# A hybrid encoder on one core: the second tokens' norm into each mixer is split into x times norm weight ahead of the root and a scaling behind it

## The chip, the cores and the metric

The kernel runs on one core of a Trainium2 chip. The metric is the device time of one execution in microseconds; the time before is the median of three runs.

## What is computed

Two layers over 256 tokens of width 1024, in float32. Each layer is a half-weighted SwiGLU feed-forward (FFN), a mixer with two head groups, and a second FFN; each of the three starts with a root-mean-square norm of the residual `x`:

```python
def rms_norm(x, g):
    x32 = x.astype(jnp.float32)
    y = x32 * lax.rsqrt(jnp.mean(x32 * x32, axis=-1, keepdims=True) + EPS)
    return (y * g.astype(jnp.float32)).astype(x.dtype)

for l in range(DEPTH):
    x = x + FFN_RES * swiglu(rms_norm(x, ffn1_norm[l]), ...)
    h = rms_norm(x, mix_norm[l])
    proj = h @ w_in[l]          # recurrent input, gate, q, k, v
    y = concat(rms_norm(y_rec, ...), rms_norm(y_att, ...))
    x = x + y @ w_out[l]
    x = x + FFN_RES * swiglu(rms_norm(x, ffn2_norm[l]), ...)
return rms_norm(x, final_norm)
```

`y_rec` is a gated linear recurrence over the tokens behind a short convolution, `y_att` windowed attention with four query heads per key head.

## The kernel before, in words

The 256 tokens are two tiles of 128, t = 0 and t = 1; the residual stays in SBUF as `xt[0]`, `xt[1]` of 128x1024. Every float32 product is made of three products of rounded parts: a tile is split into a high part (`xh`, `wh`, a rounding copy by ScalarE) and a low part (`xl`, `wl`, a subtraction by VectorE), and TensorE multiplies high by high, high by low and low by high. Weights come by SyncE's DMAs as raw 1 MB pieces; `prep_one` (L307, L308) splits them into ring slots, a 128x1024 copy on ScalarE and a 128x1024 subtraction on VectorE for each slot, some pieces ahead of their use.

The program is a chain of six stages (FFN, mixer, FFN, twice), and `boundary` joins each to the next. It runs the last part of the old stage's down projection (`tail`) for t = 0, then for t = 1, and puts in between, in this order:

- for t = 0: `evac` adds the finished PSUM halves to `xt[0]` (VectorE, L801 after an FFN), `squares` sums the squares of each half (ScalarE, L519, which writes the squares into the norm's own output tile `xn` as waste), `norm` forms the root (`rstd_of`: VectorE L506, then a power on GpSimd L509) and the normed tile in four 128x256 pieces, x times root times norm weight (VectorE, L526);
- `transposes(0)`: eight 128x128 transposes on TensorE (L544) into two PSUM banks, four high-part copies on ScalarE (L549), four low-part subtractions on VectorE (L551), each for two of the eight 128-wide column blocks k;
- the same for t = 1, then `head(0)`, `transposes(1)`, `head(1)` of the new stage. A mixer's `head` is `natural` (L561): 24 matmuls, three passes over the eight blocks; the first two passes read high parts, the third reads the low parts.

Behind the boundary the mixer goes through a list of steps written out by hand (`ORDER`): projections of 24 matmuls (L569 to L571) with a convolution behind four of them (`conv`, L888 to L891 on VectorE, then L899, L900), the recurrence's gates (L911 to L926), attention logits with a fused add and maximum (L985, L988 on VectorE) and exponentials (L990). The projections and logits share four PSUM banks, `ps_c` and `ps_g` with two buffers each.

TensorE's, SyncE's and GpSimd's instructions run in the order in which the program writes them. Those of ScalarE and VectorE are put in order by a scheduler that goes by its own estimate of when each could start. All of one engine's instructions then run in that fixed order. The pool of `xn` has one buffer, so the tile of t = 1 takes the place of that of t = 0, and whoever writes it waits until `transposes(0)` has read it.

Of the kernel before, what the change touches and what calls it, by code (L numbers as in the profile page):

```python
# [10 lines left out]
AF = mybir.ActivationFunctionType  # L11
ALU = mybir.AluOpType
# [4 lines left out]
DM = 1024  # L17
# [24 lines left out]
MAHEAD = 5  # L42
# [25 lines left out]
def encoder_kernel(  # L68
# [31 lines left out]
    pe, act, dve, pool = nc.tensor, nc.scalar, nc.vector, nc.gpsimd  # L100
# [216 lines left out]
    def prefetch(target):  # L317
        while state["half"] <= min(target, state["cap"], len(halves) - 1):
            j = state["half"]
            n = turns.get(halves[j][0], 0)  # L320
            if n >= SLOTS and ring[n - SLOTS] not in used:
                return
            with ExitStack() as behind:
                for ins in state["behind"]:
                    behind.enter_context(tc.issue_after(ins.ins))
                prep_one()
# [13 lines left out]
    xt = [res_p.tile([128, DM], F32, name=f"x{t}", tag=f"x{t}") for t in range(2)]  # L340
# [12 lines left out]
    gain_t = {}  # L353

    def load_gain(i):
        if i < len(gains):
            g = a_p.tile([128, DM], F32, tag="a", name="gain")
            nc.sync.dma_start(out=g, in_=gains[i].partition_broadcast(128))
            gain_t[i] = g
# [26 lines left out]
    def setup_early():  # L386
        idle = ep_p.tile([128, T], F32R, tag="th", name="idle")
        dve.memset(idle.bitcast(F32), 0.0)
        pi = bank("b")

        def keep_warm(n):
            for _ in range(n):
                pe.matmul(pi[:, 0:T], idle[:, 0:128], idle, start=True, stop=True)

        dve.memset(half_t, -0.5)
        dve.memset(ones_t, 1.0)
        load_x(0)
        rows8 = xn_p.tile([128, DM], F32, tag="xn", name="rows8")[0:KD, 0:128]
        nc.scalar.dma_start(out=rows8, in_=ffn1_norm[0].rearrange("(k c) -> k c", c=128))
        nc.scalar.dma_start(out=eye_t, in_=eye)  # L400
        ps = bank("b")
        keep_warm(WARM)
        pe.transpose(ps[:, 0:KD], rows8, eye_t[0:KD, 0:KD])
        keep_warm(WARM2)
        dve.tensor_copy(out=gcol, in_=ps[:, 0:KD])
# [93 lines left out]
    xn_t = {}  # L499
# [3 lines left out]
    def rstd_of(ss, n):  # L503
        st = st_p.tile([128, 2], F32, tag="rstd", name="rstd")
        if n == 2:
            dve.tensor_scalar(st[:, 0:1], ss[:, 0:1], ss[:, 1:2], EPS, ALU.add, ALU.add)  # L506
        else:
            dve.tensor_scalar(st[:, 0:1], ss[:, 0:1], EPS, None, ALU.add)
        pool.tensor_tensor(out=st[:, 1:2], in0=st[:, 0:1], in1=half_t, op=ALU.pow)  # L509
        return st[:, 1:2]  # L510

    ss_t = {}

    def squares(t, hf):
        if hf == 0:
            ss_t[t] = st_p.tile([128, 2], F32, tag="ss", name="ss")
            xn_t[t] = xn_p.tile([128, DM], F32, tag="xn", name="xn")
        sl = slice(hf * 512, hf * 512 + 512)
        return act.activation(out=xn_t[t][:, sl], in_=xt[t][:, sl], func=AF.Square,  # L519
                              scale=1.0 / math.sqrt(DM), accum_out=ss_t[t][:, hf:hf + 1])  # L520

    def norm(t, gi):
        r = rstd_of(ss_t[t], 2)
        for c in range(0, DM, 256):
            sl = slice(c, c + 256)
            ins = dve.scalar_tensor_tensor(out=xn_t[t][:, sl], in0=xt[t][:, sl], scalar=r, in1=gain_t[gi][:, sl],  # L526
                                           op0=ALU.mult, op1=ALU.mult)
        return ins

    def new_x():  # L530
# [3 lines left out]
    def transposes(t):  # L534
        if t == 0:
            new_x()
        xn = xn_t.pop(t)
        ts_ = slice(t * 128, (t + 1) * 128)
        parts = []
        for hf in range(2):  # L540
            ps = bank("ab"[t])
            for j in range(4):
                k = hf * 4 + j
                pe.transpose(ps[:, j * 128:(j + 1) * 128], xn[:, k * 128:(k + 1) * 128], eye_t)  # L544
                if j % 2:
                    p3 = ps[:, (j - 1) * 128:(j + 1) * 128].rearrange("p (k c) -> p k c", k=2)
                    parts.append((p3, cur["h"][:, k - 1:k + 1, ts_], cur["l"][:, k - 1:k + 1, ts_]))
        for p3, xh, xl in parts:
            i1 = act.activation(out=xh, in_=p3, func=AF.Copy)  # L549
        for p3, xh, xl in parts:  # L550
            i2 = dve.tensor_sub(out=xl, in0=p3, in1=xh.bitcast(F32))  # L551
        return [i1, i2]
# [41 lines left out]
    def front():  # L594
        return tc.high_priority(offset=FRONT)

    def boundary(tail, evac, gi, head, ahead):
        prefetch(ahead)
        state["cap"] = ahead
        state["ahead"] = AHEAD  # L600
        tail(0, 0)
        with front():
            for hf in range(2):
                evac(0, hf)
                squares(0, hf)
            norm(0, gi)
        tail(1, 1)
        with front():
            evac(1, 0)
            transposes(0)  # L610
            squares(1, 0)
        tail(1, 2)
        with front():
            evac(1, 1)
            i1 = squares(1, 1)
            i2 = norm(1, gi)
        prefetch(ahead)
        state["behind"] = [i1, i2]
        state["cap"] = ahead + EARLY
        prefetch(ahead + FORCE)  # L620
        head(0)
        with front():
            state["behind"] = transposes(1)
        state["cap"] = 1 << 30
        prefetch(ahead + FORCE2)
        head(1)
        state["behind"] = []
        if gi % 3 != 1:
            load_gain(gi + 1)
# [61 lines left out]
    def ffn(st, acc_done):  # L691
        gu_ps = {}
        hh_t = {}
        acc = {}
# [139 lines left out]

        if st == (DEPTH - 1, 2):
            tail, evac = dn_cols, acc
        return head if st != (0, 0) else first_head, body, tail, evac

    def mix(l):
        st = (l, 1)  # L840
# [295 lines left out]
                if n == "D":  # L1136
                    load_gain(3 * l + 2)

        return head, body, tail, evac

    engines = mybir.EngineType
    with tc.manual_schedule(engines={engines.PE, engines.SP, engines.Pool}):
        stages = [ffn((0, 0), None)]
        step = {"s": first_squares, "n": first_norm, "T": first_transposes, "m": stages[0][0]()}
        for n, f in (("h", first_split), ("w", first_prep)):
            step[n] = lambda *a, f=f: f(False, *a)
            step[n.upper()] = lambda *a, f=f: f(True, *a)
        with tc.manual_schedule(engines={engines.Activation, engines.DVE}):
            setup_early()
            for _ in range(RAWS + 2):  # L1150
                load_raw()
            for tok in FIRST:
                ins = step[tok[0]](*map(int, tok[1:]))
                if tok in BEHIND:
                    state["behind"].append(ins)
        prefetch(3 + LEAD)
        state["behind"] = [ins]
        prefetch(3 + LEAD2)
        state["behind"] = []
        for s in range(3 * DEPTH):  # L1160
            _, body, tail, evac = stages[s]
            body()
            n = s + 1
            if n == 3 * DEPTH:
                with tc.manual_schedule(engines={engines.Activation, engines.DVE}):
                    finish(tail, evac)
                break
            stages.append(mix(n // 3) if n % 3 == 1 else ffn((n // 3, n % 3), None))
            first = index[(n // 3, n % 3), "kv", 0] if n % 3 == 1 else index[(n // 3, n % 3), "gu", 0]
            boundary(tail, evac, n, stages[n][0], first + (MAHEAD if n % 3 == 1 else 3))  # L1170


_INS = ['x', 'ffn1_norm', 'ffn1_w_gate', 'ffn1_w_up', 'ffn1_w_down', 'mix_norm', 'w_in', 'conv_w', 'conv_b',
# [43 lines left out]
```

## Time and profile before

| | |
|---|---|
| median of 3 runs | 938.15 us (937.98 to 938.85) |
| the profiled execution | 938.13 us, of it 936.4 us in the span |
| TensorE (PE) busy | 926.0 us, 99% of the span |
| VectorE (DVE) busy | 696.8 us, 74% |
| ScalarE (ACT) busy | 544.4 us, 58% |
| GpSimd (POOL) busy | 37.4 us, 4% |
| granted TensorE clock, mean | 0.997 of full speed |

Times in the rows are microseconds from the span's start. PEld is TensorE's weight load, which overlaps the matmuls (PE). A row of the timeline gives start, duration of one or of a merged run, engine, line, operation, output and inputs, shape, count, and in brackets how long the engine idled just before and what released it. A duration overlaps the next instruction's by a little, so distances between starts are shorter than durations.

### The profile page before, as it was taken

The numbers are of one execution on the slowest core, as the hardware profiler recorded it, in microseconds if no ns is written. First come the engines' busy times: TensorE is split into PE (matmuls) and PEld (weight loads), VectorE is DVE, ScalarE is ACT, GpSimd is POOL, SyncE is SP. The second block draws the span as 40 slices with busy tenths as digits, with TensorE's granted clock in tenths as the row PEclk, the third lists the DMA queues.
The fourth block names the chain that finished last, engine by engine and source line by source line (L and its number), as shares of the span: only waits on it lengthen the run. The fifth ranks groups of instructions, "written<-read, shape, count | busy, mean of one in ns | idle before, by whom it ended". The sixth has DMA issues, their size and how long they took to land.

```text
span 936.4 us, 13679 instructions
## 1 busy us (share of the span) xinstructions
PE 926.0 (99%) x5288; PEld 804.9 (86%) x5288; DVE 696.8 (74%) x1213; ACT 544.4 (58%) x1005; POOL 37.4 (4%) x60
## 2 busy tenths in 40 slices
PE   9999999999999999999999999999999999999997
PEld 8888888889988888888888888888999888888885
DVE  6888666769998876666688666666799887666663
ACT  7665555548855655555466555554687575555542
POOL 2300000000010000000030000000000100000000
PEclk9999999999999999999999999999999999999998
DMA  9786956714255755565557666555162576665521
GB/s 310 223 269 219 314 184 203 233 56 151 75 162 201 261 186 180 185 205 195 173 175 237 188 196 195 187 180 180 51 221 68 180 240 202 195 195 181 183 87 45
DMA packets 125009, 172.54 MB, mean 184 GB/s; under 512 B 3925, under 2 KB 108797, under 8 KB 124944
## 3 DMA queue, kind: packets, MB, share of 16 engines
q1 hardware_dynamic: 122192, 166.21, 54.8%
q0 software_dynamic: 2304, 4.87, 1.6%
q8 instruction: 41, 0.67, 0.3%
q10 hardware_dynamic: 448, 0.59, 0.2%
q14 instruction: 24, 0.20, 0.1%
HBM read 170.59 MB, written 3.16 MB: 186 GB/s over the span
## 4 chain that ended last, share of the span: by engine, by line
PE 95%; DVE 2%; ACT 1%; issue 1%; DMA 1%; POOL 0%; SPq 0%; POOLq 0%; DVEq 0%
PE ps_g L581 16%; PE ps_c L581 16%; PE ps_c L580 7%; PE ps_g L580 7%; PE ps_a L590 5%; PE ps_a L592 4%; PE ps_a L591 4%; PE ps_b L591 4%; PE ps_b L592 4%; PE ps_b L590 4%; PE ps_g L706 2%; PE ps_c L706 2%; PE ps_a L1021 1%; PE ps_g L569 1%; PE ps_g L570 1%; PE ps_g L571 1%
## 5 line engine op out<-in xcount | busy, mean ns | idle before, releaser
L308 DVE TENSOR_TENSOR wl<-raw,wh 128x1024 fp32r<-128x1024 f32 (+1 forms) x320 | 367.3, 1156 | 102.3 <-ACT wh L307 98.0
L307 ACT ACTIVATE wh<-raw 128x1024 fp32r<-128x1024 f32 (+1 forms) x306 | 301.9, 999 | 82.8 <-PE ps_b L592 60.5
L581 PE MATMUL ps_c<-xhl,wh 128*128 128x512 f32 x640 | 231.3, 396 | 0.0
L581 PE MATMUL ps_g<-xhl,wh 128*128 128x512 f32 x640 | 231.3, 396 | 0.0
L580 PE MATMUL ps_c<-xhl,wl 128*128 128x256 f32 x560 | 156.2, 279 | 0.0
L580 PE MATMUL ps_g<-xhl,wl 128*128 128x256 f32 x560 | 156.1, 279 | 0.0
L581 PEld LDWEIGHTS ps_c<-xhl,wh 128*128 128x128 f32 x640 | 120.1, 188 | 23.0
L581 PEld LDWEIGHTS ps_g<-xhl,wh 128*128 128x128 f32 x640 | 120.1, 188 | 23.0
L580 PEld LDWEIGHTS ps_c<-xhl,wl 128*128 128x128 f32 x560 | 105.6, 189 | 3.5
L580 PEld LDWEIGHTS ps_g<-xhl,wl 128*128 128x128 f32 x560 | 105.6, 188 | 3.5
L590 PE MATMUL ps_a<-wh,hh 128*128 128x512 f32 x168 | 65.7, 391 | 0.0
L590 PE MATMUL ps_b<-wh,hh 128*128 128x512 f32 x168 | 65.6, 391 | 0.0
L592 PE MATMUL ps_b<-wh,hl 128*128 128x512 f32 x168 | 65.4, 389 | 0.0
L591 PE MATMUL ps_b<-wl,hh 128*128 128x512 f32 x168 | 65.4, 389 | 0.0
L592 PE MATMUL ps_a<-wh,hl 128*128 128x512 f32 x168 | 65.4, 389 | 0.0
L591 PE MATMUL ps_a<-wl,hh 128*128 128x512 f32 x168 | 65.4, 389 | 0.0
L766 ACT ACTIVATE sg<-ps_g 128x256 f32<-128x256 f32 x40 | 15.4, 385 | 63.3 <-PE ps_g L581 63.3
L766 ACT ACTIVATE sg<-ps_c 128x256 f32<-128x256 f32 x40 | 15.3, 383 | 52.5 <-PE ps_c L581 51.6
L767 DVE TENSOR_TENSOR sg<-ps_g,sg 128x256 f32<-128x256 f32 x40 | 17.0, 425 | 32.8 <-ACT sg L766 32.7
L766 ACT ACTIVATE su<-ps_c 128x256 f32<-128x256 f32 x40 | 15.4, 386 | 39.0 <-PE ps_c L581 39.0
L754 ACT ACTIVATE hh<-th 128x256 fp32r<-128x256 f32 x80 | 33.4, 417 | 8.1 <-DVE th L748 7.8
L591 PEld LDWEIGHTS ps_a<-wl,hh 128*128 128x128 f32 x168 | 31.6, 188 | 6.9
(323 smaller groups left out, 1577.9 us busy)
## 6 DMA issues: line engine op xcount, KB each, us to landing
raw<-in_ffn_w_down_dram SPq DMA_DIRECT2D x44, 1024.0 KB, 5.0
raw<-in_ffn_w_gate_dram SPq DMA_DIRECT2D x43, 1024.0 KB, 5.4
raw<-in_ffn_w_up_dram SPq DMA_DIRECT2D x43, 1024.0 KB, 5.4
raw<-in_w_in_dram SPq DMA_DIRECT2D x14, 1024.0 KB, 5.5
raw<-in_w_out_dram SPq DMA_DIRECT2D x8, 1024.0 KB, 7.0
lb<-ld POOLq DMA_DIRECT2D x1, 2048.0 KB, 14.9
bias_t<-lb POOLq DMA_DIRECT2D x1, 1536.0 KB, 12.4
gain<-in_ffn_norm_dram SPq DMA_DIRECT2D x3, 512.0 KB, 4.6
```

What stands on the lines that cost most here:

```text
L307: act.activation(out=h3, in_=src, func=AF.Copy)
L308: dve.tensor_sub(out=l3, in0=src, in1=h3.bitcast(F32))
L569: pe.matmul(dst, wh[:, ks], xh[:, k, t0:t1], start=(k == 0), stop=False)
L580: pe.matmul(dst[:, 0:T], wl[:, ks], x2[:, 0, k, :], start=False, stop=False)
L581: pe.matmul(dst, wh[:, ks], x2[:, :, k, :], start=(k == 0), stop=(k == KD - 1))
L590: pe.matmul(acc[hf], ah[:, ts_], wh[:, cs], start=first, stop=False)
L591: pe.matmul(acc[hf], ah[:, ts_], wl[:, cs], start=False, stop=False)
L592: pe.matmul(acc[hf], al[:, ts_], wh[:, cs], start=False, stop=last)
L706: pe.matmul(ps, x, w[k // 2][p % 2][:, k % 2 * 512:k % 2 * 512 + 512], start=(p == 0 and k == 0), stop=(p == 2 and k == KD - 1))
L754: act.activation(out=hh, in_=src, func=AF.Copy)
L766: act.activation(out=s, in_=ps[:, T:2 * T], func=AF.Copy)
L767: dve.tensor_tensor(out=s, in0=ps[:, 0:T], in1=s, op=ALU.add)
```

## The change

It applies at the two boundaries into a mixer alone (`gi % 3 == 1`), and to t = 1 alone. The squares of t = 1 are written as waste into the PSUM bank whose contents `evac` has just taken out, no longer into `xn`. After each half's `evac`, `gained_x` (L532) forms x times norm weight for that half, 128x512, into `xn`. When the root is there, `norm_gained` scales `xn` in place: three 128x256 pieces on VectorE (L539), the fourth on ScalarE (L541). In all other places `norm` stays. The numbers behind the diff's functions move by 14 to 20 lines in the changed kernel: L549 is L563 there, L551 is L565, L801 is L821, L888 to L891 are L908 to L911, L985 is L1005, L988 is L1008.

```diff
-    def squares(t, hf):
+    def squares(t, hf, junk=None):
...
-        return act.activation(out=xn_t[t][:, sl], in_=xt[t][:, sl], func=AF.Square,
+        return act.activation(out=xn_t[t][:, sl] if junk is None else junk, in_=xt[t][:, sl], func=AF.Square,
                               scale=1.0 / math.sqrt(DM), accum_out=ss_t[t][:, hf:hf + 1])
...
+    def gained_x(t, gi, hf):
+        sl = slice(hf * 512, hf * 512 + 512)
+        dve.tensor_tensor(out=xn_t[t][:, sl], in0=xt[t][:, sl], in1=gain_t[gi][:, sl], op=ALU.mult)
+
+    def norm_gained(t):
+        r = rstd_of(ss_t[t], 2)
+        for c in range(0, DM, 256):
+            o = xn_t[t][:, c:c + 256]
+            if c < DM - 256:
+                ins = dve.tensor_scalar(o, o, r, None, ALU.mult)
+            else:
+                act.activation(out=o, in_=o, func=AF.Copy, scale=r)
         return ins
...
-    def boundary(tail, evac, gi, head, ahead):
+    def boundary(tail, evac, gi, head, ahead, acc):
...
-            squares(1, 0)
+            squares(1, 0, acc and acc[1][0])
+            if acc:
+                gained_x(1, gi, 0)
         tail(1, 2)
         with front():
             evac(1, 1)
-            i1 = squares(1, 1)
-            i2 = norm(1, gi)
+            i1 = squares(1, 1, acc and acc[1][1])
+            if acc:
+                gained_x(1, gi, 1)
+                i2 = norm_gained(1)
+            else:
+                i2 = norm(1, gi)
...
-            boundary(tail, evac, n, stages[n][0], first + (MAHEAD if n % 3 == 1 else 3))
+            boundary(tail, evac, n, stages[n][0], first + (MAHEAD if n % 3 == 1 else 3), acc if n % 3 == 1 else None)
```

What this does to the order is seen on VectorE at the boundary into the first mixer. Before (x_115 is `xt[0]`, x_116 is `xt[1]`; xhl holds the high and low parts of the transposed tile, those of t = 0 come from ps_a and those of t = 1 from ps_b; wl is the low part of a ring slot):

```order
L801 SCALAR_TENSOR_TENSOR x_116<-ps_b,x_116 128x512
L526 SCALAR_TENSOR_TENSOR xn<-x_115,rstd,gain 128x256 x4
L551 TENSOR_TENSOR xhl<-ps_a,xhl 128x2x128 x2
L801 SCALAR_TENSOR_TENSOR x_116<-ps_b,x_116 128x512
L551 TENSOR_TENSOR xhl<-ps_a,xhl 128x2x128 x2
L506 TENSOR_SCALAR rstd<-ss 128x1
L526 SCALAR_TENSOR_TENSOR xn<-x_116,rstd,gain 128x256 x4
L308 TENSOR_TENSOR wl<-raw,wh 128x1024
L551 TENSOR_TENSOR xhl<-ps_b,xhl 128x2x128 x4
```

With the change, the same place:

```order
L821 SCALAR_TENSOR_TENSOR x_116<-ps_b,x_116 128x512
L526 SCALAR_TENSOR_TENSOR xn<-x_115,rstd,gain 128x256 x4
L532 TENSOR_TENSOR xn<-x_116,gain 128x512
L565 TENSOR_TENSOR xhl<-ps_a,xhl 128x2x128
L821 SCALAR_TENSOR_TENSOR x_116<-ps_b,x_116 128x512
L565 TENSOR_TENSOR xhl<-ps_a,xhl 128x2x128
L532 TENSOR_TENSOR xn<-x_116,gain 128x512
L506 TENSOR_SCALAR rstd<-ss 128x1
L565 TENSOR_TENSOR xhl<-ps_a,xhl 128x2x128
L539 TENSOR_SCALAR xn<-xn,rstd 128x256 x3
L308 TENSOR_TENSOR wl<-raw,wh 128x1024
L565 TENSOR_TENSOR xhl<-ps_a,xhl 128x2x128
```

The four low-part subtractions of t = 0 stood in pairs ahead of L506; now they stand one by one, and the last of them is behind the three scalings and the 128x1024 weight subtraction. At the boundary into the second mixer the rows from L532 on are the same; ahead of them, before and now, the four L526 stand before the L801 (L821).

On ScalarE, with the change, in the same boundary (L307 copies a ring slot's high part):

```order
L519 ACTIVATE xn,ss<-x_115 128x512 x2
L519 ACTIVATE ps_b,ss<-x_116 128x512
L563 ACTIVATE xhl<-ps_a 128x2x128 x4
L519 ACTIVATE ps_b,ss<-x_116 128x512
L307 ACTIVATE wh<-raw 128x1024
L541 ACTIVATE xn<-xn,rstd 128x256
L563 ACTIVATE xhl<-ps_b 128x2x128 x4
```

Before, both squares of t = 1 stood together behind the four copies from ps_a; the first now stands ahead of them, and the scaling of the fourth piece stands behind the weight copy.

Further on in the mixer the scheduler also sets a few instructions of VectorE in another order. The place at the third convolution, before (pr, stm: attention logits and their maximum, of which the second row of each pair, with stm alone, is the read of the maximum; xc: the convolution, which reads the projection's bank ps_c):

```order
L988 TENSOR_SCALAR stn<-stm 128x2
L888 TENSOR_SCALAR xc<-ps_c,par 128x256
L308 TENSOR_TENSOR wl<-raw,wh 128x1024
L890 SCALAR_TENSOR_TENSOR xc<-ps_c,par,xc 128x254
L985 ISA pr,stm<-ps_g,bias_t,sink_t 128x256
L985 ISA stm 128x1
L890 SCALAR_TENSOR_TENSOR xc<-ps_c,par,xc 128x255
L985 ISA pr,stm<-ps_g,bias_t,sink_t 128x256
L985 ISA stm 128x1
L891 SCALAR_TENSOR_TENSOR xc<-ps_c,par,xc 128x255
```

With the change, the same place, where the weight subtraction L308 stands just ahead of the first row:

```order
L1008 TENSOR_SCALAR stn<-stm 128x2
L908 TENSOR_SCALAR xc<-ps_c,par 128x256
L1005 ISA pr,stm<-ps_g,bias_t,sink_t 128x256
L1005 ISA stm 128x1
L910 SCALAR_TENSOR_TENSOR xc<-ps_c,par,xc 128x254
L1005 ISA pr,stm<-ps_g,bias_t,sink_t 128x256
L1005 ISA stm 128x1
L910 SCALAR_TENSOR_TENSOR xc<-ps_c,par,xc 128x255
L1008 TENSOR_SCALAR stn<-stm 128x2
L1005 ISA pr,stm<-ps_c,bias_t,sink_t 128x256
L1005 ISA stm 128x1
L911 SCALAR_TENSOR_TENSOR xc<-ps_c,par,xc 128x255
```

One more logits pair and one more L1008 now stand ahead of the convolution's last instruction. TensorE's, GpSimd's and SyncE's instructions stand as before.

## Rows read from the trace of the kernel before

**Rows 1.** The page, engines over the span: busy time, share, instructions
```profile
PE 926.0 (99%) x5288; PEld 804.9 (86%) x5288; DVE 696.8 (74%) x1213; ACT 544.4 (58%) x1005; POOL 37.4 (4%) x60
```

**Rows 2.** Busy time by stretch: both boundaries, the first mixer's two early stretches
```profile
core 0: us, PE busy (x) PEld busy (x) DVE busy (x) ACT busy (x) POOL busy (x), PEclk, DMA share, GB/s
188.00:206.00 18.00, 17.53 (x108) 15.10 (x107) 12.23 (x26) 7.63 (x20) 1.12 (x2) 1.00 0.01 3
206.00:230.00 24.00, 23.96 (x204) 23.23 (x203) 20.61 (x50) 17.59 (x42) 0.00 (x0) 1.00 0.52 175
230.00:262.00 32.00, 32.00 (x279) 31.27 (x278) 31.80 (x76) 25.92 (x63) 0.00 (x0) 1.00 0.26 89
647.00:665.00 18.00, 17.51 (x109) 15.11 (x109) 12.97 (x27) 8.57 (x21) 1.12 (x2) 1.00 0.02 5
```

**Rows 3.** Timeline of the first boundary, up to the root of t = 1
```profile
195.96 1.03 PE L544 MATMUL ps_a<-eye_t,xn 128*128 128x128 f32 x8
196.59 1.21 ACT L549 ACTIVATE xhl<-ps_a 128x256 fp32r<-128x256 f32 x4 [3.75 <-PE ps_a L544]
197.28 0.76 DVE L551 TENSOR_TENSOR xhl<-ps_a,xhl 128x256 fp32r<-128x256 f32 x2 [0.90 <-ACT xhl L549]
197.96 0.68 DVE L801 SCALAR_TENSOR_TENSOR x<-ps_b,x 128x512 f32<-128x512 f32 x1
198.55 0.75 DVE L551 TENSOR_TENSOR xhl<-ps_a,xhl 128x256 fp32r<-128x256 f32 x2
199.30 1.04 ACT L307 ACTIVATE wh<-raw 128x1024 fp32r<-128x1024 f32 x1
199.43 0.21 DVE L506 TENSOR_SCALAR rstd<-ss 128x1 f32<-128x1 f32 x1
199.77 0.54 PEld L561 LDWEIGHTS ps_c<-w_i,xhl 128*128 128x128 f32 x4
```

**Rows 4.** The same timeline, from the norm of t = 1 on
```profile
200.31 1.67 DVE L526 SCALAR_TENSOR_TENSOR xn<-x,rstd,gain 128x256 f32<-128x256 f32 x4 [0.66 <-POOL rstd L509]
200.91 0.54 PEld L544 LDWEIGHTS ps_b<-eye_t,xn 128*128 128x128 f32 x4 [0.60 <-ACT wh L307]
200.94 1.53 PE L544 MATMUL ps_b<-eye_t,xn 128*128 128x128 f32 x8 [0.42 <-DVE xn L526]
201.90 1.22 DVE L308 TENSOR_TENSOR wl<-raw,wh 128x1024 fp32r<-128x1024 f32 x1
202.95 0.57 PEld L561 LDWEIGHTS ps_c<-w_i,xhl 128*128 128x128 f32 x4 [0.21 <-ACT xhl L549]
204.86 0.54 PEld L561 LDWEIGHTS ps_c<-w_i,xhl 128*128 128x128 f32 x4
205.33 0.19 PEld L569 LDWEIGHTS ps_g<-xhl,wh 128*128 128x128 f32 x1
```

**Rows 5.** Instructions of the new kinds elsewhere: count, then ns min/median/max
```profile
L653 DVE TENSOR_TENSOR xn<-x,gain x3: 425/682/692, 921.8 to 928.9; 128x512 f32<-128x512 f32 x2, 128x256 f32<-128x256 f32 x1
L666 ACT ACTIVATE xn<-xn,rstd x2: 709/716/722, 927.9 to 931.3; 128x512 f32<-128x512 f32 x2
```

**Rows 6.** Timeline: four scalings of 128x256 on VectorE in the first norm
```profile
6.39 1.15 DVE L418 TENSOR_SCALAR xn<-x,rstd 128x256 f32<-128x256 f32 x4 [0.67 <-POOL rstd L509]
```

**Rows 7.** Timeline: transposes of t = 1 that wait for nothing, at a boundary into an FFN
```profile
291.26 1.02 PEld L544 LDWEIGHTS ps_b<-eye_t,xn 128*128 128x128 f32 x8
292.12 1.21 ACT L549 ACTIVATE xhl<-ps_b 128x256 fp32r<-128x256 f32 x4
```

**Rows 8.** Timeline of the third convolution in the first mixer
```profile
225.17 1.23 DVE L308 TENSOR_TENSOR wl<-raw,wh 128x1024 fp32r<-128x1024 f32 x1 [0.17 <-ACT wh L307]
226.70 0.47 DVE L985 CUSTOM_DVE_ANT_0 pr<-ps_g,bias_t,sink_t 128x256 f32<-128x256 f32 x1
227.10 0.48 DVE L890 SCALAR_TENSOR_TENSOR xc<-ps_c,par,xc 128x255 f32<-128x255 f32 x1
228.43 0.19 PEld L569 LDWEIGHTS ps_c<-xhl,wh 128*128 128x128 f32 x1 [0.24 <-DVE xc L891]
```

**Rows 9.** Chain of waits at the second boundary: start, us, what
```profile
659.12 0.49 DVE xn L526
659.75 0.74 PE ps_b L544 x4
```

More of the change, by code (lines that the diff above doesn't have):

```diff
@@ L527, in norm @@
                                            op0=ALU.mult, op1=ALU.mult)
+        return ins
+    def gained_x(t, gi, hf):
[9 more added lines that the diff above has]
+                act.activation(out=o, in_=o, func=AF.Copy, scale=r)
         return ins
@@ L836, in ffn @@
             tail, evac = dn_cols, acc
-        return head if st != (0, 0) else first_head, body, tail, evac
+        return head if st != (0, 0) else first_head, body, tail, evac, acc
     def mix(l):
@@ L1137, in body @@
                     load_gain(3 * l + 2)
-        return head, body, tail, evac
+        return head, body, tail, evac, None
     engines = mybir.EngineType
@@ L1160, in encoder_kernel @@
         for s in range(3 * DEPTH):
-            _, body, tail, evac = stages[s]
+            _, body, tail, evac, acc = stages[s]
             body()
```

## The prediction

> **What bounds the kernel now.** I read the page's engine shares first: TensorE is busy for 926.0 of 936.4 us [rows 1]. So nothing is won beside it, and what makes it wait is lost in full, unless a later wait takes it up. Next I read the busy time by stretch around the two places that the change touches [rows 2]. In each boundary into a mixer TensorE is idle for only 0.47 and 0.49 of 18 us. In the mixer behind it there is next to no idle time (23.96 of 24 us, then 32.00 of 32), and VectorE is almost full there (31.80 of 32), while in the boundary it works 12.23 of 18. The reader should see from this that little can be gained, and that VectorE has room in the boundary if its instructions stand in the right order.
>
> Then the timeline of the first boundary [rows 3, 4]. The waits of t = 1 follow one another: L506 at 199.43, then the power on GpSimd, the first L526 at 200.31, and the transposes at 200.94, which TensorE had waited 0.42 us for. They then come in the time of the L526 pieces (1.53 us for eight; 1.02 to 1.03 where nothing is awaited [rows 7], [rows 3]), and the head behind them waits another 0.21 us. If all this went, 0.47 + 0.50 + 0.21, so 1.2 us at a boundary and 2.4 us in all, would be the most that the change can win. The second boundary has the same distances (L526 to the transposes: 0.63 us in both [rows 4, 9]).
>
> **The change, part by part.** I replay the new order of VectorE with the distances between starts of the first boundary.
>
> *The two products ahead of the root.* One product of 128x512 costs about 0.60 us from start to start: it lasts 0.682 to 0.692 us [rows 5], as L801 does, whose successor starts 0.59 us later [rows 3]. The first must wait until the transposes of t = 0 have read `xn`: 195.96 + 1.03 = 197.0. It is followed by the first subtraction L565 at 197.6, which takes 0.35 (two from 197.28 to the next row at 197.96), so the second evacuation starts at 197.95: before, 197.96. Squares and their sum are not late by this; before, VectorE sat idle here for 0.90 us, and that covers the first product. Then L565 at 198.55, the second product at 198.9, L506 at 199.5 instead of 199.43. From L506 to the scaling stay 0.88 us (199.43 to 200.31), so the scaling starts at 200.4, late by 0.1.
>
> *The scaling.* Four scalings take 1.15 us in the first norm [rows 6], so 0.27 a piece: the three end their turn at 201.2, where the four L526 ended theirs at 201.90. The fourth, on ScalarE, stands behind the weight copy L307, which is over at 199.30 + 1.04 = 200.34, so the root lets it start at about 200.45. For 128x512 such a scaling takes 0.71 us [rows 5], so for half of it between 0.36 and 0.71: done by 201.2 at the latest. So all of `xn` is there by about 201.3 instead of 201.98. That is the gain that stands to be had, 0.7 us of it.
>
> *What stands behind the scaling now.* The last of the four subtractions of t = 0 gives the low part of blocks 6 and 7, which the last two matmuls of `head(0)` read. Before, it was over at 199.30 [rows 3], and TensorE came to these matmuls at about 200.3 (the group of four loads from 199.77 lasts 0.54). Now it stands behind the scalings and behind the weight subtraction L308: 201.2, plus 1.15 (1.22 less the overlap [rows 4]), gives a start at 202.35; with the 0.42 that one lasts it is over at 202.8. TensorE stands from 200.3 to 202.8, since the transposes of t = 1 come behind `head(0)` in its program: their first load moves from 200.91 to about 203.1, by 2.2 us. What is queued there is the transposes, then `head(1)`, then the whole mixer.
>
> *What comes back.* The transposes then run without gaps. In the boundary into an FFN the first high-part copy starts 0.86 us after the first load and the fourth ends 1.21 us later [rows 7]; then 18 of the 24 matmuls are left, at 0.1175 (a group of four in 0.47: 204.86 to 205.33). That is 0.86 + 1.21 + 2.1 = 4.2 us to the mixer's first projection; where the two loads ahead of them have nothing queued it may be 4.0. Before, it was 4.42 (200.91 to 205.33). So 203.1 + 4.1 = 207.2 against 205.33: **1.85 us lost at each boundary**, with bounds of 1.6 and 2.1, or **3.7 us** for the two.
>
> *In the mixer.* The evacuation of the third convolution's bank is what TensorE waits 0.24 us for [rows 8]. One more logits reduction, 0.40 us from start to start (226.70 to 227.10), and one small L1008 (below 0.15) now stand ahead of it, while the 0.17 us that L308 waited for ScalarE may go. So 0.3 us more a mixer; bounds are 0 (VectorE gains time while TensorE stands) and 0.7. In all **0.6 us**.
>
> *At nothing:* the squares into PSUM (ScalarE idles for 3.75 us ahead of the copies from ps_a [rows 3]; where they come late, in the second boundary, since the norm of t = 0 stands ahead of the evacuation there, the copies slip a little, beside the tail's last three matmuls); the weight DMA behind the boundary, requested later by as much as TensorE; the boundaries out of the mixers, where the evacuations only change places.
>
> Sum: 3.7 + 0.6 = 4.3 us on the profiled execution's 938.13, which stands 0.02 below the median of 938.15: **942.4 us**.
>
> The replay hangs on VectorE keeping its order. The subtraction L551 of 198.55 was ready at 197.80, when the four copies ended, and still ran behind L801 [rows 3]. The Trainium skill, "PSUM — Partial Sum Buffer", section "Engine vs sequencer instructions", says that the queues of ScalarE, VectorE and GpSimd are strictly first in, first out. By that rule the sum stands; were overtaking possible, the last subtraction would slip in ahead of the scaling and the first rival would hold. The row above agrees with the rule.
>
> **The rivals.** *First, not slower: the last subtraction comes in time, and the shorter scaling is won.* It needs that subtraction done by 200.3; from there on the root decides. The transposes would start at about 200.85, follow the pieces at 0.27 instead of 0.40, and the head would end earlier by 0.4 to 0.6 us, so 1.0 in all: 937.1 us, or up to 940 if the subtraction is late by a part. For it speaks that VectorE has room in the stretch [rows 2] and that the pieces do pace the transposes [rows 4]; against it, the written order. The Trainium skill, "Perfetto Trace Analysis", section "Optimizing Scalar/DVE Operations", says that breaking up instructions may let work be done sooner where VectorE is not full but holds up another engine. By that rule it is this rival that comes about; the trace agrees with both conditions (12.23 of 18 us, and TensorE's 0.42), but no row shows a split that was free of a new order.
>
> *Second, slower still: the new order costs more in the mixers.* VectorE is full there [rows 2], and each convolution frees a bank that TensorE wants soon. If a weight subtraction (1.22 us) gets ahead of such a convolution where none was, with no slack to hide it, a mixer loses 1.2 instead of 0.3 us: 942.4 + 1.8 = 944.2. For it speaks that the wait at the third convolution has no slack already [rows 8]; against it, that there the weight subtraction stood ahead before, too.
>
> **How the numbers follow.** A change of 0.2%, about 1.9 us, is what a measurement of this kernel can tell from none. The forecast has a chance of 0.75 and by its bounds reaches from 938.13 + 3.2 = 941.3 to 938.13 + 5.6 = 943.7. The second rival has 0.14, the first 0.11, of which 0.02 lie beyond 0.2% faster (the most that can be won, 2.4 us, gives 935.7) and 0.07 within 0.2%; the rest of it is above 940.0. So faster 0.02, same 0.07, slower 0.91. I take a little of that back, 0.03 from slower to same, for a stall that the mixers take up in a way I do not see. The range from 940.2 to 944.3 leaves out the first rival and the upper part of the second.
>
> **What would show it.** Right: in both boundaries VectorE's last subtraction from ps_a starts about 202.3 in the first boundary's time, TensorE waits some 2.5 us inside `head(0)` for that line (not for the scaling), the transposes of t = 1 then take about 1.0 us instead of 1.5, and the mixer's first projection starts 1.6 to 2.1 us later. TensorE's idle time between 188 and 206 us rises from 0.47 to about 2.5 to 3 us. Wrong: the wait at the transposes stays on the scaling, or the subtraction runs ahead of the weight subtraction; or the boundary loses what I say and the mixer ends no later than before. If the wait at the third convolution is no longer than 0.24 us, the 0.6 us were wrong; if it is over 1 us, the second rival holds.

## The result, and the profile after

The changed kernel takes **946.19 us** (median of three, 946.14 to 947.72) against 938.15: a ratio of 1.0090, 95% interval 1.0077 to 1.0104. It is slower by 8.0 us, where 4.3 were forecast, and lies above the range given. The profiled execution is the longest of the three, 947.72 us, with 945.9 in the span.

The engines over its span, as [rows 1]:

```profile
PE 929.3 (98%) x5288; PEld 807.8 (85%) x5288; DVE 697.0 (74%) x1215; ACT 545.8 (58%) x1007; POOL 37.5 (4%) x60
```

TensorE has the same 5288 matmuls but is busy for 3.3 us more: some of them ran slower. Busy time by stretch, as [rows 2] (stretch, length, busy time of each engine, PEclk, DMA share, GB/s; the second boundary now comes later):

```profile
188.00:206.00 18.00, 15.75 (x88) 13.55 (x87) 12.13 (x28) 8.30 (x21) 1.11 (x2) 0.95 0.01 4
206.00:230.00 24.00, 23.79 (x198) 23.05 (x198) 17.49 (x37) 14.80 (x33) 0.00 (x0) 0.97 0.49 170
230.00:262.00 32.00, 30.52 (x262) 29.45 (x262) 31.68 (x79) 27.00 (x68) 0.00 (x0) 1.00 0.22 72
652.00:673.00 21.00, 18.72 (x107) 16.54 (x106) 13.62 (x28) 8.72 (x22) 1.11 (x2) 0.92 0.06 15
```

TensorE is idle for 2.25 of the first 18 us (before: 0.47; 2.5 to 3 were forecast) and for 1.48 of the 32 us inside the mixer (before: 0). And PEclk, 1.00 in all four stretches before, is 0.95, 0.97 and 0.92 around the boundaries.

VectorE at the first boundary, as [rows 3, 4] (start, duration, engine, line, operation, what it waited for):

```profile
199.59 0.41 DVE L565 TENSOR_TENSOR xhl<-ps_a,xhl 128x256 fp32r<-128x256 f32 x1
200.33 0.88 DVE L539 TENSOR_SCALAR xn<-xn,rstd 128x256 f32<-128x256 f32 x3 [0.33 <-POOL rstd L509]
201.13 1.21 DVE L308 TENSOR_TENSOR wl<-raw,wh 128x1024 fp32r<-128x1024 f32 x1
202.26 0.41 DVE L565 TENSOR_TENSOR xhl<-ps_a,xhl 128x256 fp32r<-128x256 f32 x1
```

The scaling starts at 200.33 and the last low-part subtraction of t = 0 at 202.26; the replay had said 200.4 and 202.35. TensorE's weight loads there, as [rows 4]:

```profile
202.73 0.30 PEld L575 LDWEIGHTS ps_c<-w_i,xhl 128*128 128x128 f32 x2 [2.38 <-DVE xhl L565]
202.97 0.90 PEld L558 LDWEIGHTS ps_b<-eye_t,xn 128*128 128x128 f32 x8
...
204.93 0.97 PEld L575 LDWEIGHTS ps_c<-w_i,xhl 128*128 128x128 f32 x4
205.78 0.97 PEld L575 LDWEIGHTS ps_c<-w_w,xhl 128*128 128x128 f32 x4
...
208.51 0.19 PEld L583 LDWEIGHTS ps_g<-xhl,wh 128*128 128x128 f32 x1
```

TensorE stands for 2.38 us on the subtraction, as forecast, and the transposes come at 202.97 (forecast: 203.1). But a group of four loads of `head(1)` then takes 0.85 us from start to start instead of 0.47, until 208. The windows of 1 us say why (same columns as above):

```profile
203.00:204.00 1.00, 1.00 (x10) 0.87 (x9) 0.00 (x0) 0.29 (x2) 0.00 (x0) 1.00 0.00 0
204.00:205.00 1.00, 0.96 (x6) 0.85 (x5) 0.60 (x2) 1.00 (x5) 0.00 (x0) 0.60 0.00 0
205.00:206.00 1.00, 1.00 (x7) 1.00 (x7) 0.93 (x4) 0.86 (x1) 0.00 (x0) 0.50 0.03 8
206.00:207.00 1.00, 1.00 (x6) 1.00 (x6) 1.00 (x1) 0.00 (x0) 0.00 (x0) 0.50 0.06 16
207.00:208.00 1.00, 1.00 (x8) 1.00 (x7) 0.12 (x1) 0.00 (x0) 0.00 (x0) 0.69 0.00 0
```

The granted clock fell to half, 1.2 of 2.4 GHz, behind the stall, and stayed there for about 3.4 us. The second boundary shows the same (0.71, 0.50, 0.50, 0.58 from 668 to 672).

The third convolution of the first mixer, as [rows 8], on ScalarE, VectorE and TensorE:

```profile
227.37 1.06 ACT L307 ACTIVATE wh<-raw 128x1024 fp32r<-128x1024 f32 x1 [1.18 <-DMA raw<-in_w_in_dram]
228.46 1.23 DVE L308 TENSOR_TENSOR wl<-raw,wh 128x1024 fp32r<-128x1024 f32 x1 [0.55 <-ACT wh L307]
229.67 0.54 DVE L908 TENSOR_SCALAR xc<-ps_c,par 128x256 f32<-128x256 f32 x1
232.19 0.47 DVE L911 SCALAR_TENSOR_TENSOR xc<-ps_c,par,xc 128x255 f32<-128x255 f32 x1
232.72 0.19 PEld L583 LDWEIGHTS ps_c<-xhl,wh 128*128 128x128 f32 x1 [1.13 <-DVE xc L911]
```

Before, the convolution's first operation (L888 at 224.46) stood ahead of the weight subtraction L308. Now all of it stands behind L308, and so behind a weight DMA that had not landed. TensorE waits 1.13 us for the bank; before, 0.24. The waits of its weight loads in the whole first mixer (line, waited for, us in total, times, longest):

```profile
PEld ps_c L583 <- DVE xc L911: 1.1, 1, 1.1
PEld ps_c L583 <- DVE ge L963: 0.7, 1, 0.7
PEld ps_g L583 <- ACT i_t L940: 0.4, 1, 0.4
PEld ps_c L998 <- DVE ql_t L1136: 0.2, 1, 0.2
```

Two more banks, those of the gelu product (L963) and of the recurrence's gate (L940), are waited for, and a logits operand (L1136) for 0.2 us; before, the same view has of all these only the convolution's bank, at 0.24.

In the second mixer the same weight piece is there in time. The wait at the third convolution there, before and after:

```profile
687.24 0.19 PEld L569 LDWEIGHTS ps_c<-xhl,wh 128*128 128x128 f32 x1 [0.25 <-DVE xc L891]
```

```profile
696.09 0.19 PEld L583 LDWEIGHTS ps_c<-xhl,wh 128*128 128x128 f32 x1 [0.50 <-DVE xc L911]
```

The waits on L963, L940 and L1136 are 0.7, 0.4 and 0.2 us there too. What the first of them comes from is seen on VectorE, before and after:

```profile
709.91 0.40 DVE L943 SCALAR_TENSOR_TENSOR ge<-x,ps_c 128x256 f32<-128x256 f32 x1
710.22 0.69 DVE L935 TENSOR_TENSOR_SCAN i_t<-a_t,i_t 128x256 f32<-128x256 f32 x1
```

```profile
718.88 0.66 DVE L955 TENSOR_TENSOR_SCAN i_t<-a_t,i_t 128x256 f32<-128x256 f32 x1
719.46 0.39 DVE L963 SCALAR_TENSOR_TENSOR ge<-x,ps_c 128x256 f32<-128x256 f32 x1
719.90 0.19 PEld L583 LDWEIGHTS ps_c<-xhl,wh 128*128 128x128 f32 x1 [0.73 <-DVE ge L963]
```

The product that frees the bank stood ahead of the recurrence's second scan (L935); now it stands behind it (L955), and TensorE waits 0.73 us. So the new order is not one of a few instructions at the third convolution: it has other places on VectorE, and on ScalarE inside the mixers too.

### The profile page after: what moved, and what is told of

It reads as the page before. It is cut to its first block, busy times and chain, and to the rows that moved or that the text cites. A ratio compares the mean times of both kernels' runs of the same rounds, so it can differ in the third digit from the quotient of the medians.

```text
span 945.9 us, 13675 instructions
## 1 busy us (share of the span) xinstructions
PE 929.3 (98%) x5288; PEld 807.8 (85%) x5288; DVE 697.0 (74%) x1215; ACT 545.8 (58%) x1007; POOL 37.5 (4%) x60
## 4 chain that ended last, share of the span: by engine, by line
PE 90%; DVE 5%; ACT 2%; issue 1%; DMA 1%; POOL 0%; POOLq 0%; DVEq 0%
PE ps_g L595 16%; PE ps_c L595 16%; PE ps_g L594 7%; PE ps_c L594 7%; PE ps_a L604 4%; PE ps_a L606 4%; PE ps_a L605 4%; PE ps_b L605 4%; PE ps_b L606 4%; PE ps_b L604 4%; PE ps_g L726 2%; PE ps_c L726 2%; PE ps_c L575 1%; PE ps_c L597 1%; PE ps_g L597 1%
## 5 line engine op out<-in xcount | busy, mean ns | idle before, releaser
L308 DVE TENSOR_TENSOR wl<-raw,wh 128x1024 fp32r<-128x1024 f32 (+1 forms) x320 | 367.0, 1156 | 103.4 <-ACT wh L307 98.7
L307 ACT ACTIVATE wh<-raw 128x1024 fp32r<-128x1024 f32 (+1 forms) x306 | 302.2, 1000 | 86.4 <-PE ps_b L606 59.8
```

What stands on the lines that cost most here:

```text
L307: act.activation(out=h3, in_=src, func=AF.Copy)
L308: dve.tensor_sub(out=l3, in0=src, in1=h3.bitcast(F32))
```

## The experiments

Three marks on TensorE sum up every run: the first load of `transposes(0)`, the first load of the mixer's first projection, and the first load of the next FFN's `transposes(0)`. From the first to the second is the boundary, from the second to the third the mixer. All from the profiled executions, in us:

| kernel | boundary 1 | mixer 1 | boundary 2 | mixer 2 |
|---|---|---|---|---|
| before | 9.60 | 78.91 | 9.60 | 78.89 |
| after (947.72) | 12.82 | 80.70 | 12.86 | 80.09 |
| after, again (946.15) | 11.40 | 80.92 | 12.57 | 80.08 |
| weight subtraction behind | 10.26 | 81.04 | 10.25 | 80.11 |
| scalings behind too | 9.17 | 78.89 | 9.16 | 78.89 |
| order alone | 14.52 | 80.68 | 13.54 | 80.09 |
| stall filled, 18 matmuls | 11.39 | 80.10 | 11.39 | 80.11 |

For "after" the four differences sum to 3.22 + 1.79 + 3.26 + 1.20 = 9.5 of the 9.6 us that this execution is longer.

The theory: the whole loss hangs on the place of one subtraction in VectorE's queue, by three ways: TensorE stands for it; the clock falls behind the stall; and the scheduler puts another order into the mixers. (That it does so because it estimates TensorE later is an inference; no run shows its estimates.) The rivals stand in the expectations.

**The weight subtraction behind the last low part.** Of the changed kernel's order, only this pair is swapped in each boundary; the mixers' orders are those of the changed kernel.

```diff
-            transposes(0)
+            subs = transposes(0)
...
-        state["behind"] = [i1, i2]
+        state["behind"] = [i1, i2] + (subs if acc else [])
```

> The changed kernel with one swap on VectorE at each boundary into a mixer: the last low-part subtraction of t = 0 stands ahead of the 128x1024 weight subtraction, still behind the three scalings; every other order, in the mixers too, is the changed kernel's. Theory A (the loss is the late subtraction's stall, the halved TensorE clock behind it, and the mixers' new order, 1.8 and 1.2 us): the subtraction is over at about 201.55, the wait falls from 2.4 to about 1.2 us, the clock stays full, 0.6 us stay lost at each boundary and 3.0 us in the mixers, so about 942.3. Rival C (the mixers lose only as an after-effect of the stall, not by their order): the mixers lose nothing, about 939.3. Rival B (the split itself costs, in work and in ScalarE's quarter): over 943.

Measured: 942.71 us (942.41 to 942.84), ratio 1.0048 (1.0034 to 1.0062). The stall and the transposes behind it:

```profile
201.64 0.30 PEld L575 LDWEIGHTS ps_c<-w_i,xhl 128*128 128x128 f32 x2 [1.24 <-DVE xhl L565]
201.88 0.90 PEld L558 LDWEIGHTS ps_b<-eye_t,xn 128*128 128x128 f32 x8
```

A stall of 1.24 us is left, the clock stays at 1.00, and each boundary costs 0.65 us instead of 3.2. But the mixers still cost 2.13 and 1.22 us, no less than behind the longer stall: their new order is a loss of its own, and not an after-effect of the stall or of the fall.

**The scalings behind the subtractions too.** Both low-part subtractions of blocks 4 to 7 now come ahead of the scaling, as before the change. The order in the mixers then comes out as it was before the change.

```diff
-    def norm_gained(t):
+    def norm_gained(t, last):
...
-                ins = dve.tensor_scalar(o, o, r, None, ALU.mult)
+                with tc.issue_after(last.ins):
+                    ins = dve.tensor_scalar(o, o, r, None, ALU.mult)
```

(with `last=subs[1]`, and the edit above)

> The split as in the changed kernel, but the scalings and the weight subtraction are queued behind the last low-part subtraction of t = 0; with this the order in the mixers comes out as in the kernel before. Theory A: no stall, full clock, the mixers as before, and the shorter scaling is won: 0.4 to 0.6 us at each boundary, so about 937.1. Rival B (the split itself costs): over 943. Rival C says the same as A here.

Measured: 937.29 us (937.24 to 938.37), ratio 0.9992 (0.9983 to 1.0001). VectorE and TensorE at the first boundary:

```profile
199.58 0.74 DVE L566 TENSOR_TENSOR xhl<-ps_a,xhl 128x256 fp32r<-128x256 f32 x2
200.32 0.88 DVE L540 TENSOR_SCALAR xn<-xn,rstd 128x256 f32<-128x256 f32 x3
```

```profile
200.74 1.24 PE L559 MATMUL ps_b<-eye_t,xn 128*128 128x128 f32 x8
204.85 0.19 PEld L584 LDWEIGHTS ps_g<-xhl,wh 128*128 128x128 f32 x1
```

The scaling is not late at all (200.32), since the two subtractions fit into the wait for the root. The transposes take 1.24 us instead of 1.53 and no longer wait for VectorE ahead of them (before: 0.42 us); TensorE still stands 0.25 us in `head(0)` for a low-part subtraction. Each boundary wins 0.43 us, the mixers lose nothing. So by the marks the split itself gains 0.9 us, though the interval of this run still reaches 1.0001; all that the changed kernel lost came from the order.

**The order alone.** The kernel before, without the split, with the last low-part subtraction held back until the boundary's weight subtraction has been issued. In the traces the mixers' order on VectorE and ScalarE is that of the changed kernel.

```diff
         for p3, xh, xl in parts:
...
+        for p3, xh, xl in held:
+            with tc.issue_after(state["sub"].ins):
+                dve.tensor_sub(out=xl, in0=p3, in1=xh.bitcast(F32))
```

> The kernel before, without the split, but the last low-part subtraction of t = 0 is queued behind the 128x1024 weight subtraction at each boundary into a mixer; the order in the mixers then comes out nearly as in the changed kernel. Theory A: the norm's four pieces end later than the three scalings, so the wait is 3.1 us instead of 2.4, the clock is halved behind it, the mixers lose as in the changed kernel: 946.2 + 1.4 = 947.6. Rival B (the split is what costs): within 3 us of the kernel before, about 941.

Measured: 948.89 us (948.52 to 949.85), ratio 1.0113 (1.0097 to 1.0128). The stall, then the window of 1 us in which the clock falls and the first one at half clock (columns as above):

```profile
203.35 0.50 PEld L563 LDWEIGHTS ps_c<-w_i,xhl 128*128 128x128 f32 x2 [3.42 <-DVE xhl L626]
203.79 1.66 PEld L544 LDWEIGHTS ps_b<-eye_t,xn 128*128 128x128 f32 x8
```

```profile
202.00:203.00 1.00, 0.00 (x0) 0.00 (x0) 1.00 (x2) 0.00 (x0) 0.00 (x0) 0.84 0.00 0
203.00:204.00 1.00, 0.65 (x3) 0.65 (x4) 0.29 (x1) 0.00 (x0) 0.00 (x0) 0.50 0.00 0
```

Without any new operation, the one late subtraction costs even more than the change: four L526 pieces stand ahead of it instead of three shorter scalings, the stall is 3.42 us, and the clock, which falls before the stall is over, is at half for some 6.8 us, until 209.5. The mixers lose 1.77 and 1.20 us, as in the changed kernel.

**The stall filled.** The changed kernel with 18 matmuls of 128x256 put into the stall of `head(0)`. They write a spare bank that nobody reads; ScalarE's and VectorE's orders are those of the changed kernel.

```diff
+                if t == 0 and p == 2 and k == 6:
+                    warm = bank("a")[:, 0:256]
+                    for _ in range(FILL):
+                        pe.matmul(warm, xh[:, 0, ts_], ws[0][0][0][:, 0:256], start=True, stop=True)
```

> The changed kernel with 18 more matmuls (128 columns of the high part against 256 weight columns, into a bank nobody reads) on TensorE ahead of the two matmuls that wait for the late subtraction; all of VectorE's and ScalarE's order is the changed kernel's. They run while TensorE would stand still. Theory A: the stall stays as long, but the clock stays full, and the 1.5 us that the halved clock cost at each boundary come back: about 943.2. Rival (the halved clock costs nothing that is not waited for anyway): 946 to 947.

Measured: 943.99 us (943.93 to 944.11), ratio 1.0062 (1.0048 to 1.0076).

```profile
200.19 2.19 PEld L577 LDWEIGHTS ps_a<-w_w,xhl 128*128 128x128 f32 x18
202.64 0.30 PEld L580 LDWEIGHTS ps_c<-w_i,xhl 128*128 128x128 f32 x2 [0.26 <-DVE xhl L566]
202.88 0.90 PEld L559 LDWEIGHTS ps_b<-eye_t,xn 128*128 128x128 f32 x8
...
206.99 0.19 PEld L588 LDWEIGHTS ps_g<-xhl,wh 128*128 128x128 f32 x1
```

The transposes come no earlier than in the changed kernel (202.88 against 202.97), yet the projection comes at 206.99 instead of 208.51, because the clock stayed at 1.00. So the fall is worth 11.39 against 12.82, 1.4 us a boundary. In its first mixer the weight copy at the third convolution did not wait for its DMA:

```profile
224.59 1.06 ACT L308 ACTIVATE wh<-raw 128x1024 fp32r<-128x1024 f32 x1
```

and TensorE's wait there is 0.4 instead of 1.1 to 1.3 us. That is most of the difference between 1.19 us in the first mixer here and 1.77 to 2.13 in the kernels of the table whose mixers have this order too. In the second mixer all of them lose 1.19 to 1.22.

**The changed kernel again**, with more executions.

> The changed kernel itself again, with more executions, to see how much of its median the halved clock behind the stalls makes. Its two executions without a profile took 946.14 and 946.19 us at a mean granted clock of 0.997, the profiled one 947.72 at 0.994. Theory A (both boundaries fall to half clock in every execution; the profiled one only lost a little more): every execution between 946 and 948, the mean clock lower than that of the kernel before by 0.002 to 0.004 on this chip, so 0.994 to 0.997 where the kernel before shows 0.998 to 0.999. Theory B (the fall belongs to the profiled execution alone, and the executions without it lose their time elsewhere): a mean clock equal to that of the kernel before in most executions, with the same 946.2 us.

Measured: 947.48 us (946.15, 947.06, 947.91, 948.07), ratio 1.0099 (1.0084 to 1.0115), at mean clocks of 0.997, 0.995, 0.994 and 0.994; the kernel before had 0.997 to 0.999 on that chip. This time the profiled execution is the shortest. Its first boundary and then its second:

```profile
202.79 0.30 PEld L575 LDWEIGHTS ps_c<-w_i,xhl 128*128 128x128 f32 x2 [2.38 <-DVE xhl L565]
203.03 0.90 PEld L558 LDWEIGHTS ps_b<-eye_t,xn 128*128 128x128 f32 x8
...
207.15 0.19 PEld L583 LDWEIGHTS ps_g<-xhl,wh 128*128 128x128 f32 x1
```

```profile
665.46 0.30 PEld L575 LDWEIGHTS ps_c<-w_i,xhl 128*128 128x128 f32 x2 [2.38 <-DVE xhl L565]
665.70 1.62 PEld L558 LDWEIGHTS ps_b<-eye_t,xn 128*128 128x128 f32 x8
...
670.99 0.19 PEld L583 LDWEIGHTS ps_g<-xhl,wh 128*128 128x128 f32 x1
```

The same stall of 2.38 us left the clock at 1.00 at the first boundary and halved it at the second. So theory A was too strict: the fall does not come at each stall of this length. The execution with one fall took 946.15 us, the one with two 947.72. The two executions of the first measurement at 946.14 and 946.19 us, with the same span and clock as this one, were most likely of the first kind, and those of 947.91 and 948.07, at a mean clock of 0.994, of the second; no trace shows them, and 947.06 at 0.995 lies between. No trace shows an execution of this kernel without a fall.

**Half the filling.** As the filled kernel, with 9 matmuls.

> As the run with 18 filling matmuls in each stall, with 9 instead: TensorE then stands about 1.2 us at a boundary instead of 2.3 or 0.3, until the same subtraction of VectorE. Theory A (what counts for the clock is how long TensorE stands, and a stand of 1.2 us brings no fall, as the run with the weight subtraction behind showed): granted clock 1.00 behind the stall, 944.0 us (943.6 to 944.5), no other than with 18. Rival C (any stand in front of the transposes halves the clock in this order of VectorE): about 946, with windows of 0.50 behind the boundaries.

Measured: 945.14 us (944.45 to 945.80), ratio 1.0072 (1.0058 to 1.0086). The clock stays at 1.00 behind stalls of 1.3 us, as expected, and boundary and mixer are those of the filled kernel (11.40 and 80.08 at the first). The time is 1.1 us longer all the same, above the 943.6 to 944.5 that were expected, and in the trace this lies elsewhere: TensorE stands still once in the second layer's first FFN, far from any edit,

```profile
501.46 0.19 PEld L600 LDWEIGHTS ps_g<-xhl,wh 128*128 128x128 f32 x1 [1.06 <-PE ps_c L600]
```

where the filled kernel has no such gap. What it waited for stays open.

**All four scalings on VectorE**, otherwise as the kernel with the scalings behind the subtractions, **and that kernel again** beside it.

```diff
-            if c < DM - 256:
-                with tc.issue_after(last.ins):
-                    ins = dve.tensor_scalar(o, o, r, None, ALU.mult)
-            else:
-                act.activation(out=o, in_=o, func=AF.Copy, scale=r)
+            with tc.issue_after(last.ins):
+                ins = dve.tensor_scalar(o, o, r, None, ALU.mult)
```

> As the kernel with the scalings behind the subtractions, but with all four 128x256 scalings on VectorE and none on ScalarE: what does ScalarE's quarter bring? The fourth scaling starts 0.27 us behind the third, and the transposes of its two blocks wait for it. Theory A (the scalings pace the transposes): 0.1 to 0.3 us later at each boundary, 937.3 + 0.2 to 0.6 = 937.5 to 937.9 us. Rival D (the last pair of transposes comes behind it anyway): 937.3.

> The kernel with the scalings behind the subtractions again, beside the one with four scalings on VectorE and on the same chip: 937.3 us (937.0 to 937.8), 0.9 us below the kernel before; the rival says that the 0.9 us were chance, and then it is within 0.3 us of the kernel before.

Measured: 937.33 us (937.05 to 937.93), ratio 0.9989 (0.9981 to 0.9998), and 937.30 us (937.19 to 937.94), ratio 0.9991 (0.9982 to 0.9999), against 938.23. ScalarE's quarter brings nothing: with VectorE's fourth piece, too, the eight transposes last 1.24 us, and the boundary is 9.15 us against 9.17. The gain of 0.9 us is there again, with both intervals just below 1. With either scaling this is the best version found, but the gain is half of the 0.2% that the prediction had set as the least that can be told from no change.

## Why the prediction was wrong

*The boundary's stall: right.* The order was read rightly, VectorE kept it, and the times of the replay hold within 0.15 us. Where the clock did not fall, the projection came at 207.15 us, forecast 207.2; the boundary lost 1.80 us, forecast 1.85. The Trainium skill, "PSUM — Partial Sum Buffer", section "Engine vs sequencer instructions", says that VectorE's queue is strictly first in, first out. The trace agrees: the four copies of t = 0 were over at 196.55 + 1.21 = 197.8, and the last subtraction still ran at 202.26, behind the scalings and L308.

*What failed first: "18 of the 24 matmuls are left, at 0.1175".* That duration was taken from a TensorE that had not stood. It was carried across a stall of 2.4 us without asking whether it holds behind one. It does at one boundary of one trace, and not at three of the four traced. The missing term is 1.2 to 1.5 us for each fall: one in the execution of 946.15 us, two in the profiled one. A hint lay in the trace of before, at its end, which the prediction does not read:

```profile
930.00:932.00 2.00, 0.00 (x0) 0.00 (x0) 0.91 (x3) 1.09 (x3) 0.55 (x1) 0.91 0.11 42
932.00:934.00 2.00, 0.00 (x0) 0.00 (x0) 0.05 (x1) 0.02 (x1) 0.00 (x0) 0.50 0.67 238
```

TensorE has no matmul from 930 us on, and the clock (after the five engines) is at 0.50 from 932. A stall of 2.5 us was foreseen, and this row says that one of about that length may not be free of it.

*What failed second, and weighs more: the 0.3 us a mixer.* It was taken as one more logits reduction less a wait that "may go". It measured 1.2 us a mixer, and 1.8 to 2.0 in the first. At the third convolution itself the 0.3 us were right where the weight piece was there in time: 0.50 us instead of 0.25 in the second mixer. What had no term are the other places of the new order, waits of 0.7 us on L963 and 0.4 on L940; only one place of the mixer had been replayed, and ScalarE's order there not at all. Why L940 comes to be waited for stays open. And "the weight DMA, requested later by as much as TensorE" at nothing was wrong: the convolution's first operation changed sides with L308 (L888 stood ahead of it, L908 stands behind it), so that the whole convolution inherits each wait of the weight piece, ScalarE's copy and behind it the DMA, which lands 6.7 us after its issue in this trace. This makes 0.6 to 0.9 us of the first mixer's loss.

By the marks of the execution of 946.15 us, the boundaries lost 1.80 + 2.97 = 4.8 us where 3.7 were forecast, and the mixers 2.01 + 1.19 = 3.2 where 0.6 were. Of the 3.7 us that are missing, the boundaries are thus 1.1, all of it the fall, and the mixers 2.6.

*The rivals.* The second rival, a weight subtraction ahead of a convolution at 1.2 us a mixer, has the measured size of a mixer without the late DMA, but by luck: its mechanism makes 0.25 us of the 1.2, and the rest are waits that no rival names. Its sign, a wait of over 1 us at the third convolution, came in the first mixer (1.13), where the DMA was late, and not in the second (0.50). The argument against it, "there the weight subtraction stood ahead before, too", was true only of the convolution's later operations. The first rival is what the kernel becomes once the order is mended: 937.3 us, where 937.1 was worked out. The Trainium skill, "Perfetto Trace Analysis", section "Optimizing Scalar/DVE Operations", says that breaking up instructions may let work be completed sooner where VectorE is not saturated but holds up another engine. The trace of that kernel agrees: the same split, 0.43 us sooner at each boundary. In the changed kernel's order it was 1.8 us later, or more.

Every error went the same way, and each was a wait or a slowdown that follows from the new order, not from the new operations: the run with the order alone has them all. The upper end of the range, 944.3, took no such case in.

## What to carry to other kernels

Where a scheduler orders the queues, a small edit is three things: its own cost, the place of everything around it, and a new order further on, since later places follow from estimated times. Read the order of every engine at every place where the bounding engine had no slack before, and for each instruction that changed sides with a long one ask what that one waits for. Where the edit makes TensorE stand, look at the granted clock behind it: here, behind 2.38 us, a fall cost 1.2 to 1.5 us on top of the 1.8 that the boundary lost without one. And a split that loses may win with one instruction moved: with the last low-part subtraction put back ahead of the scalings and the weight subtraction, +8.0 us here became -0.9.

## What the runs showed of the hardware

- Behind stalls of TensorE of 1.24 to 1.32 us the granted clock stayed at 1.00 (four of four in two traces); at stalls of 2.38 us it fell to 0.50 in three of four, each time for some 3.4 us, which cost 1.2 to 1.5 us; at stalls of 3.42 us it fell in two of two, for some 6.8 us at the first boundary and 3.4 at the second. Two executions of the same kernel thus differed by 1.6 us (946.15 and 947.72), at mean clocks of 0.997 and 0.994.
- The 1 MB weight DMA of the first mixer's third convolution landed 5.3 us after its issue in the filled kernel and 6.7 in the changed one, with the next one issued 0.94 us behind it in both. What decides this wasn't found; it is worth 0.6 to 0.9 us in the first mixer.
- Matmuls that nobody needs, put into the stall, went with a clock of 1.00: 18 of 128x256 in each stall gave 943.99 us, against 946.19 and 947.48 without them; 0.6 to 0.9 us of this is the DMA that was not late.
